# Keys of two latent-attention heads from one product

## The chip, the cores and the metric

The kernel runs on one core of one Trainium2 chip. The metric is the device time of one execution in microseconds (us); lower is better. A change of about 0.5% (6.2 us) is what a measurement of this kernel can tell from no change.

## The reference, cut to what matters

The network has two layers over 256 context and 256 latent tokens, model width 1024. Each layer has three groups of heads (differential attention, multi-head latent attention, a bidirectional recurrence called HGRN2), an output projection and an MLP. The change is in the latent attention (MLA) alone: six heads, whose keys have 64 parts that are made per head from a latent of 128 numbers, and 32 rotary parts that all heads share.

```python
qu = (rmsnorm(cq, g_cq) @ w_uq).reshape(bsz, n, 6, 64 + 32)      # cq: 256 numbers a token
kvu = (rmsnorm(ckv, g_ckv) @ w_ukv).reshape(bsz, n, 6, 64 + 64)  # ckv: 128 numbers a token
q_nope, q_rope = qu[..., :64], qu[..., 64:]
k_nope, mla_v = kvu[..., :64], kvu[..., 64:]
...
s = einsum(q_nope, k_nope) + einsum(q_rope, k_rope)   # k_rope: one for all heads
p = softmax(s * 96 ** -0.5);  o = p @ mla_v
```

In the first layer 512 queries are needed, in the second (last) one only the 256 latent ones.

## The kernel before, in words

Activations lie feature-major: features on the 128 partitions, tokens along the free axis. Most products are made in three parts (`mm3`, L139 to L142): an operand x is split into a high part in the type fp32r and the rest, and high·high, high·low and low·high are added up in PSUM. So a product of 512 tokens is three matmul instructions of 512 columns. The scores (L1225), the turn of the rotary keys (L1171) and the weighting of values (L1239) are plain fp32 products; the trace has two records for each of those.

The stage at hand comes in each layer after the input projections. `do_pair(2)` projects queries and keys of the last pair of differential heads from weights that `wunit` loads into the buffers `raw` (four of them, all loads on SP's queue) and splits into `wh` (ACT, L135) and `wl` (DVE, L136). The MLA weights `w_uq` and `w_ukv` are loaded ahead of that into three of the same `raw` buffers (L1134, L1138) and split into `uqh`, `uql`, `ukh`, `ukl`. Then:

- L1171 turns the shared rotary keys `krt` to partitions 64 to 95 of a PSUM tile, four matmuls; ACT copies them into the lower part of both key buffers `mk` (L1175).
- `mla_head(hd)` (L1177) makes the 64 key parts of one head: three matmuls with 64 stationary columns over 512 tokens, and an ACT copy to `mk` (L1181). Then six matmuls make its 96 query parts, an ACT copy (L1187) takes them to `mq`, and the rotary part of the latent tokens is turned by DVE (L1190) and three POOL operations (L1191 to L1193).
- L1206 to L1208 make the values `mv` of all six heads, twelve matmuls of 384 columns.
- `da_steps` and `mla_steps` give steps of the two attentions in turn, for pairs of heads and blocks of 128 queries. The order of MLA heads is 1, 0, 3, 2, 5, 4; the next head's keys and queries are made half-way through the head before (`s.after`, L1256). A step is scores, maximum (DVE), exponential (ACT), turn (PE, L907), weighted values (L1239).

Between the steps of layer 0 stand matmuls of the modulation of later stages (`mod_group`, L392), as filling work; in layer 1 those of the output projection's last part (`proj_out`). Written order gives priorities; a scheduler that runs when the kernel is built then fixes the order of instructions on each engine.

Of the kernel before, what the change touches and what calls it, by code (L numbers as in the profile page):

```python
# [8 lines left out]
F32 = mybir.dt.float32  # L9
# [13 lines left out]
HALF_TURN = [8 * (i // 8 ^ 1) + i % 8 for i in range(32)]  # L23
# [17 lines left out]
def net(ctx: ExitStack, tc, x, c, cx, c_ctx, w_mod, b_mod, g_mix, g_mlp, w_in, w_out, da_lambda, da_subln_g,  # L41
        g_cq, g_ckv, w_uq, w_ukv, hg_lb, hg_norm_g, w_ff1, w_ff2, g_final,
        k_ident, k_cos, k_sin, k_krc, k_krs, k_mask, out):
    nc = tc.nc
    V, S, G, PE = nc.vector, nc.scalar, nc.gpsimd, nc.tensor
# [10 lines left out]
    ident = const.tile([128, 128], F32, name="ident")  # L56
# [82 lines left out]
    def mm3(ps, lh, ll, rh, rl, start, stop):  # L139
        PE.matmul(ps, lh, rh, start=start, stop=False)  # L140
        PE.matmul(ps, lh, rl, start=False, stop=False)  # L141
        PE.matmul(ps, ll, rh, start=False, stop=stop)  # L142
# [449 lines left out]
    def layer(l):  # L592
        last = l == DEPTH - 1
        T0q = 256 if last else 0
        Tq = NTOK - T0q
# [525 lines left out]
        def split(src, shape, nm):  # L1121
            a = mp.tile(shape, F32R, name=nm + "h")
            b = mp.tile(shape, F32R, name=nm + "l")
            return a, b
# [3 lines left out]
        else:  # L1128
            ukh = wp.tile([128, 1024], F32R, tag="wh", name="ukh", bufs=3)[:, 0:768]
            ukl = wp.tile([128, 1024], F32R, tag="wl", name="ukl", bufs=3)[:, 0:768]  # L1130
        uqh, uql = split(None, [128, 2, 576], "uq")
        for i in range(2):
            raw = raw_tile()[:, 0:576]
            nc.sync.dma_start(out=raw, in_=w_uq[l, 128 * i:128 * i + 128, :])  # L1134
            S.copy(out=uqh[:, i, :], in_=raw)
            V.tensor_sub(out=uql[:, i, :], in0=raw, in1=uqh[:, i, :].bitcast(F32))
        raw = raw_tile()[:, 0:768]
        nc.sync.dma_start(out=raw, in_=w_ukv[l])  # L1138
        S.copy(out=ukh, in_=raw)
        V.tensor_sub(out=ukl, in0=raw, in1=ukh.bitcast(F32))  # L1140

# [25 lines left out]
                return turns[cc][0]  # L1167

        kp = psum("sc")
        for t in range(4):  # L1170
            PE.matmul(kp[64:96, 128 * t:128 * t + 128], krt[:, t, :], ident, start=True, stop=True, tile_position=(0, 64))  # L1171
        NKB = 2
        kbufs = [mp.tile([96, 512], F32, name="mk0"), lp_.tile([128, 512], F32, tag="lat", name="mk1", bufs=3)[0:96, :]]
        for kb in kbufs:
            S.copy(out=kb[64:96, :], in_=kp[64:96, :])  # L1175

        def mla_head(hd, n):  # L1177
            kb = kbufs[n % NKB]
            ps = psum("mm")
            mm3(ps[0:64, :], ukh[:, 128 * hd:128 * hd + 64], ukl[:, 128 * hd:128 * hd + 64], ckh, ckl, True, True)  # L1180
            S.copy(out=kb[0:64, :], in_=ps[0:64, :])  # L1181
            ps = psum("mm")
            cs = slice(96 * hd, 96 * hd + 96)
            for i in range(2):
                mm3(ps[0:96, 0:Tq], uqh[:, i, cs], uql[:, i, cs], cqh[:, i, 0:Tq], cql[i][:, 0:Tq], i == 0, i == 1)
            qb = mp.tile([96, Tq], F32, tag="mq", name="mq", bufs=2)
            S.copy(out=qb[:, 0:Tq], in_=ps[0:96, 0:Tq])  # L1187
            x0 = Tq - 256
            t2 = mp.tile([96, 256], F32, tag="mt2", name="mt2", bufs=2)
            V.stream_shuffle(out=t2[64:96, :], in_=qb[64:96, x0:Tq], mask=HALF_TURN)  # L1190
            G.tensor_mul(out=t2[64:96, :], in0=t2[64:96, :], in1=sinT[64:96, :])  # L1191
            G.tensor_mul(out=qb[64:96, x0:Tq], in0=qb[64:96, x0:Tq], in1=cosT[64:96, :])
            G.tensor_add(out=qb[64:96, x0:Tq], in0=qb[64:96, x0:Tq], in1=t2[64:96, :])  # L1193
            return kb, qb

        heads = {1: mla_head(1, 0)}


        mv = mp.tile([128, 4, 384], F32, name="mv")
        uvh = ukh.rearrange("p (h e) -> p h e", h=6)[:, :, 64:128]  # L1200
        uvl = ukl.rearrange("p (h e) -> p h e", h=6)[:, :, 64:128]
        for t in range(4):
            ps = psum("mm")
            ts = slice(128 * t, 128 * t + 128)
            pv = ps[:, 0:384].rearrange("p (h e) -> p h e", h=6)
            PE.matmul(pv, ckh[:, ts], uvh, start=True, stop=False)  # L1206
            PE.matmul(pv, ckh[:, ts], uvl, start=False, stop=False)
            PE.matmul(pv, ckl[:, ts], uvh, start=False, stop=True)  # L1208
            S.copy(out=mv[:, t, :], in_=ps[:, 0:384])
# [37 lines left out]
        def mla_steps():  # L1247
            order = [1, 0, 3, 2, 5, 4]
            for p in range(3):
                res = {}  # L1250
                for h in (1, 0):
                    for qi, qt in enumerate(qtiles):
                        s = mla_step(p, h, qi, qt, res)
                        n = 2 * p + 1 - h
                        if qi == nq // 2 and n < 5:
                            s.after = lambda n=n: heads.update({order[n + 1]: mla_head(order[n + 1], n + 1)})  # L1256
                        if qi == nq - 1 and h == 0:
                            s.own = [lambda p=p, res=res: (V.reciprocal(out=res["s"], in_=res["s"]),
                                                            turn_y(3 + p, res["o"], res["s"]))]
                        yield s  # L1260
# [183 lines left out]
```

## Time and profile before

| | us |
|---|---|
| three runs | 1239.74, 1242.29, 1244.79 (median 1242.29) |
| the profiled execution | 1242.65 |
| its span in the trace | 1240.9 |
| TensorE busy | 1201.3 (97%) |
| VectorE (DVE) busy | 888.5 (72%) |
| ScalarE (ACT) busy | 584.4 (47%) |
| GpSimd (POOL) busy | 111.4 (9%) |
| attention of layer 0, in the span | about 240 to 372 |
| attention of layer 1, in the span | about 947 to 1035 |

The span is the time from the first to the last instruction of one profiled execution; 1.75 us of its time lie outside. TensorE's busy time counts the modelled ends of pipelined matmuls, so a busy engine may still wait a little.

### The profile page before, as it was taken

The numbers are of one execution on the slowest core, as the hardware profiler recorded it, in microseconds if no ns is written. First come the engines' busy times: TensorE is split into PE (matmuls) and PEld (weight loads), VectorE is DVE, ScalarE is ACT, GpSimd is POOL, SyncE is SP. The second block draws the span as 40 slices with busy tenths as digits, with TensorE's granted clock in tenths as the row PEclk, the third lists the DMA queues.
The fourth block names the chain that finished last, engine by engine and source line by source line (L and its number), as shares of the span: only waits on it lengthen the run. The fifth ranks groups of instructions, "written<-read, shape, count | busy, mean of one in ns | idle before, by whom it ended". The sixth has DMA issues, their size and how long they took to land.

```text
span 1240.9 us, 21471 instructions
## 1 busy us (share of the span) xinstructions
PE 1201.3 (97%) x8318; PEld 963.9 (78%) x8318; DVE 888.5 (72%) x1786; ACT 584.4 (47%) x1114; POOL 111.4 (9%) x156
## 2 busy tenths in 40 slices
PE   6999999999999999999999999999998998999997
PEld 4677888755568777878787877788986668999997
DVE  4675587767776997765778673796788877865864
ACT  3534344576653654211233322464347874653653
POOL 2200000221200100000000000140003421000000
PEclk9999999999999999999999999999999998999999
DMA  9631213456543346555555554233324413555662
GB/s 324 187 86 49 76 53 105 119 158 198 189 153 107 98 139 198 188 154 159 178 155 162 164 169 134 68 103 99 94 58 121 126 32 119 175 184 187 187 187 69
DMA packets 138199, 170.93 MB, mean 138 GB/s; under 512 B 10883, under 2 KB 116033, under 8 KB 138097
## 3 DMA queue, kind: packets, MB, share of 16 engines
q1 hardware_dynamic: 134816, 164.08, 43.8%
q0 software_dynamic: 2704, 4.94, 1.6%
q8 instruction: 66, 1.08, 0.4%
q10 hardware_dynamic: 576, 0.53, 0.1%
q14 instruction: 37, 0.30, 0.1%
HBM read 160.21 MB, written 1.05 MB: 130 GB/s over the span
## 4 chain that ended last, share of the span: by engine, by line
PE 85%; DVE 7%; DMA 3%; ACT 3%; POOL 1%; issue 1%; ACTq 0%; POOLq 0%; SPq 0%
PE mm L142 21%; PE mm L140 21%; PE mm L141 21%; PE sc L1239 3%; PE sc L1225 2%; PE mm L392 2%; PE tp L907 2%; PE mm L219 2%; PE mm L218 2%; PE mm L220 2%; DMA mraw<-in_w_mod_dram 2%; PE sc L797 1%; DMA raw<-in_w_in_dram 1%; PE mm L930 1%; DVE wl L136 1%; PE sc L691 1%
## 5 line engine op out<-in xcount | busy, mean ns | idle before, releaser
L135 ACT CAST wh<-raw 128x1024 fp32r<-128x1024 f32 (+2 forms) x204 | 211.0, 1035 | 315.4 <-PE mm L141 244.9
L136 DVE TENSOR_TENSOR wl<-raw,wh 128x1024 fp32r<-128x1024 f32 (+2 forms) x201 | 242.9, 1209 | 127.5 <-ACT wh L135 124.7
L140 PE MATMUL mm<-mhh,wh 128*128 128x512 f32 (+1 forms) x512 | 174.0, 340 | 0.8 <-DVE fz L336 0.8
L140 PE MATMUL mm<-fa,wh 128*128 128x512 f32 (+1 forms) x512 | 173.7, 340 | 0.0
L142 PE MATMUL mm<-mhh,wl 128*128 128x512 f32 (+1 forms) x512 | 173.0, 339 | 0.4 <-DVE wl L136 0.4
L141 PE MATMUL mm<-mhl,wh 128*128 128x512 f32 (+1 forms) x512 | 173.3, 338 | 0.0
L141 PE MATMUL mm<-fb,wh 128*128 128x512 f32 (+1 forms) x512 | 173.3, 339 | 0.0
L142 PE MATMUL mm<-fa,wl 128*128 128x512 f32 (+1 forms) x512 | 173.2, 339 | 0.0
L426 DVE SCALAR_TENSOR_TENSOR room<-raw,scm,room 128x1024 f32<-128x1024 f32 x84 | 106.4, 1287 | 39.8 <-DMA raw<-in_w_mod_dram 39.8
L140 PE MATMUL mm<-hh,wh 128*128 128x512 f32 (+1 forms) x336 | 126.7, 382 | 4.6 <-ACT hh L351 3.3
L141 PE MATMUL mm<-hl,wh 128*128 128x512 f32 (+1 forms) x336 | 126.8, 378 | 2.3 <-DVE hl L352 2.3
L142 PE MATMUL mm<-hh,wl 128*128 128x512 f32 (+1 forms) x336 | 126.8, 378 | 1.1 <-DVE wl L136 1.1
L140 PEld LDWEIGHTS mm<-mhh,wh 128*128 128x128 f32 x512 | 96.2, 188 | 15.5 <-ACT wh L135 2.5
L140 PEld LDWEIGHTS mm<-fa,wh 128*128 128x128 f32 x512 | 96.3, 188 | 14.2 <-ACT wh L135 2.5
L142 PEld LDWEIGHTS mm<-mhh,wl 128*128 128x128 f32 x512 | 96.3, 188 | 12.5 <-DVE wl L136 0.8
L142 PEld LDWEIGHTS mm<-fa,wl 128*128 128x128 f32 x512 | 96.4, 188 | 11.7
L141 PEld LDWEIGHTS mm<-fb,wh 128*128 128x128 f32 x512 | 96.5, 189 | 11.6
L141 PEld LDWEIGHTS mm<-mhl,wh 128*128 128x128 f32 x512 | 96.3, 188 | 11.2
L140 PEld LDWEIGHTS mm<-hh,wh 128*128 128x128 f32 x336 | 63.5, 190 | 15.6 <-ACT hh L351 4.2
L141 PEld LDWEIGHTS mm<-hl,wh 128*128 128x128 f32 x336 | 64.2, 191 | 14.0 <-DVE hl L352 4.1
L142 PEld LDWEIGHTS mm<-hh,wl 128*128 128x128 f32 x336 | 64.0, 191 | 13.2 <-DVE wl L136 2.0
L347 POOL TENSOR_TENSOR nt<-nt,bc 128x256 f32<-128x256 f32 x24 | 27.0, 1132 | 493.5 <-ACT bc L326 445.5
(333 smaller groups left out, 2189.8 us busy)
## 6 DMA issues: line engine op xcount, KB each, us to landing
raw<-in_w_ff_dram SPq DMA_DIRECT2D x128, 512.0 KB, 3.8
raw<-in_w_mod_dram SPq DMA_DIRECT2D x80, 512.0 KB, 3.7
raw<-in_w_in_dram SPq DMA_DIRECT2D x42, 512.0 KB, 3.8
mraw<-in_w_mod_dram SPq DMA_DIRECT2D x32, 256.0 KB, 6.0
raw<-in_w_out_dram SPq DMA_DIRECT2D x10, 512.0 KB, 3.7
raw<-in_w_in_dram SPq DMA_DIRECT2D x16, 256.0 KB, 5.1
raw<-in_w_in_dram SPq DMA_DIRECT2D x8, 384.0 KB, 3.3
K<-dah POOLq DMA_DIRECT2D x48, 64.0 KB, 2.3
```

Of the source, the lines that this page charges most:

```text
L135: S.copy(out=wh, in_=raw)
L136: (low.pop() if low else V).tensor_sub(out=wl, in0=raw, in1=wh.bitcast(F32))
L140: PE.matmul(ps, lh, rh, start=start, stop=False)
L141: PE.matmul(ps, lh, rl, start=False, stop=False)
L142: PE.matmul(ps, ll, rh, start=False, stop=stop)
L218: PE.matmul(ps, a, wh[:, k, 0:w], start=st, stop=False)
L219: PE.matmul(ps, a, wl[:, k, 0:w], start=False, stop=False)
L220: PE.matmul(ps, b, wh[:, k, 0:w], start=False, stop=sp)
L347: G.tensor_mul(out=ts, in0=ts, in1=self.bc[:, a - T0:b - T0])
L392: PE.matmul(ps[32 * j:32 * j + 32, :], scm[:, k, :], raw[:, 512 * q:512 * q + 512], start=(k == 0), stop=(k == KT - 1))
L426: V.scalar_tensor_tensor(out=acc[r], in0=raw, scalar=scm[:, k, r:r + 1], in1=acc[r], op0=ALU.mult, op1=ALU.add)
L1239: PE.matmul(op[64 * r:64 * r + 64, 0:128], v[:, j, 64 * c:64 * c + 64], PT[:, js], start=(j == 0), stop=(j == nk - 1), tile_position=(0, 6 ...
```

## The change

The keys of the two heads of a pair now come out of one product with 128 stationary columns (`mla_keys`), three matmuls for two heads. The even head has its 64 key parts on partitions 0 to 63 and the rotary part on 64 to 95, as before. The odd head has its key parts on partitions 64 to 127, its rotary part on 32 to 63, and zeros on 0 to 31; its scores are a product over 128 rows. So the rotary keys are turned twice (eight matmuls), and one more ACT copy and a clearing of 32 rows are there. The queries of an odd head are made with 128 stationary columns. For that the weights are loaded in another order of columns: each half of `w_uq` by three DMAs of pieces of 96, 32 and 64 columns, `w_ukv` by two DMAs of 64 columns a head, all keys ahead of all values; the values' weights are then one contiguous operand of 384 columns.

```diff
         for i in range(2):
             raw = raw_tile()[:, 0:576]
-            nc.sync.dma_start(out=raw, in_=w_uq[l, 128 * i:128 * i + 128, :])
+            rv = raw.rearrange("p (n f) -> p n f", n=3)
+            wv = w_uq[l, 128 * i:128 * i + 128, :].rearrange("p (n f) -> p n f", n=3)
+            for o, a, b in ((0, 0, 96), (96, 160, 192), (128, 96, 160)):
+                nc.sync.dma_start(out=rv[:, :, o:o + b - a], in_=wv[:, :, a:b])
...
         raw = raw_tile()[:, 0:768]
-        nc.sync.dma_start(out=raw, in_=w_ukv[l])
+        wv = w_ukv[l].rearrange("p (h f) -> p h f", h=6)
+        for o in (0, 384):
+            nc.sync.dma_start(out=raw[:, o:o + 384].rearrange("p (h f) -> p h f", h=6), in_=wv[:, :, o // 6:o // 6 + 64])
...
-        for t in range(4):
-            PE.matmul(kp[64:96, 128 * t:128 * t + 128], krt[:, t, :], ident, start=True, stop=True, tile_position=(0, 64))
-        NKB = 2
-        kbufs = [mp.tile([96, 512], F32, name="mk0"), lp_.tile([128, 512], F32, tag="lat", name="mk1", bufs=3)[0:96, :]]
-        for kb in kbufs:
+        for r in (64, 32):
+            for t in range(4):
+                PE.matmul(kp[r:r + 32, 128 * t:128 * t + 128], krt[:, t, :], ident, start=True, stop=True, tile_position=(0, r))
+        keven = [mp.tile([96, 512], F32, name="mk0"), lp_.tile([128, 512], F32, tag="lat", name="mk1", bufs=3)[0:96, :]]
+        kodd = mp.tile([128, 512], F32, name="mk2")
+        for kb in keven:
             S.copy(out=kb[64:96, :], in_=kp[64:96, :])
-
-        def mla_head(hd, n):
-            kb = kbufs[n % NKB]
+        S.copy(out=kodd[32:64, :], in_=kp[32:64, :])
+        V.memset(kodd[0:32, :], 0.0)
+
+        def mla_keys(p):
+
+            cs = slice(128 * p, 128 * p + 128)
             ps = psum("mm")
-            mm3(ps[0:64, :], ukh[:, 128 * hd:128 * hd + 64], ukl[:, 128 * hd:128 * hd + 64], ckh, ckl, True, True)
-            S.copy(out=kb[0:64, :], in_=ps[0:64, :])
+            mm3(ps, ukh[:, cs], ukl[:, cs], ckh, ckl, True, True)
+            S.copy(out=kodd[64:128, :], in_=ps[64:128, :])
+            S.copy(out=keven[p % 2][0:64, :], in_=ps[0:64, :])
+
+        def mla_head(hd):
+
+            p, odd = hd // 2, hd % 2
+            n, r = (128, 32) if odd else (96, 64)
             ps = psum("mm")
-            cs = slice(96 * hd, 96 * hd + 96)
+            cs = slice(192 * p + 64 * odd, 192 * p + 64 * odd + n)
...
-                            s.after = lambda n=n: heads.update({order[n + 1]: mla_head(order[n + 1], n + 1)})
+                            def after(n=n):
+                                if n % 2:
+                                    mla_keys(n // 2 + 1)
+                                heads[order[n + 1]] = mla_head(order[n + 1])
+                            s.after = after
```

How the instructions move on the engines (line numbers from L1135 on shift between the two kernels). First ACT at the start of layer 1's attention, before: `yh` is a part of the output projection's operand, `mk` with numbers 9059 and 9060 are the two key buffers, `sc` and `mm` are PSUM tiles.

```order
L1001 ACTIVATE yh<-tp,vT_91 128x256 x2
L1175 COPY mk_9059<-sc 32x512
L1181 COPY mk_9059<-mm 64x512
L1175 COPY mk_9060<-sc 32x512
L1187 COPY mq<-mm 96x256
L1209 COPY mv<-mm 128x384 x4
```

The same place of the changed kernel, where 9070 is the odd heads' buffer, 9068 and 9069 the even ones':

```order
L1001 ACTIVATE yh<-tp,vT_91 128x256 x2
L1182 COPY mk_9068<-sc 32x512
L1191 COPY mk_9070<-mm 64x512
L1182 COPY mk_9069<-sc 32x512
L1183 COPY mk_9070<-sc 32x512
L1192 COPY mk_9068<-mm 64x512
L1203 COPY mq<-mm 128x256
L1226 COPY mv<-mm 128x384 x4
```

Five copies instead of three stand ahead of the first queries' copy `mq`. Next ACT some 20 us earlier in layer 1, while HGRN2 ends and `do_pair(2)` takes its weights, as one piece of the difference: `wh` is the split of its first weights, `dah`, `rx` and `dak` are parts of the differential attention, `ktok` of HGRN2.

```order
-L135 CAST wh<-raw 128x1024
+L873 CAST dah<-dak 128x512
 L764 COPY ktok<-tp 128x256
-L873 CAST dah<-dak 128x512
-L855 ACTIVATE rx<-mm 128x256
-L853 ACTIVATE dak<-mm 128x256
+L855 ACTIVATE rx<-mm 128x256
+L135 CAST wh<-raw 128x1024
 L798 COPY obuf<-sc 128x2x128
```

The split of these weights moved behind three other ACT operations. Last PE in layer 1 where the keys and queries of head 0, the second head, are made, and the transposed probabilities `P` (differential) and `mP` (MLA) follow; before:

```order
L142 MATMUL mm<-yh,wl 128x256
L140 MATMUL mm<-ckh,ukh 64x512
L141 MATMUL mm<-ckl,ukh 64x512
L142 MATMUL mm<-ckh,ukl 64x512
L140 MATMUL mm<-cqh,uqh 96x256
L907 MATMUL tp<-ident,P 128x128 x4
L907 MATMUL tp<-ident,mP 128x128 x4
L141 MATMUL mm<-cql,uqh 96x256
L142 MATMUL mm<-cqh,uql 96x256
```

and in the changed kernel:

```order
L142 MATMUL mm<-yh,wl 128x256
L140 MATMUL mm<-cqh,uqh 96x256
L141 MATMUL mm<-cql,uqh 96x256
L142 MATMUL mm<-cqh,uql 96x256
L140 MATMUL mm<-cqh,uqh 96x256
L141 MATMUL mm<-cql,uqh 96x256
L142 MATMUL mm<-cqh,uql 96x256
L930 MATMUL mm<-K_8837,Q_8836 128x512 x2
L907 MATMUL tp<-ident,P 128x128 x4
L907 MATMUL tp<-ident,mP 128x128 x4
```

The three matmuls of the keys are gone there, and all queries of head 0 are made ahead of the turns of `P` and `mP`. Outside the two attention stages and the work just ahead of them the rows of both kernels are alike.

## Rows read from the trace of the kernel before

**Rows 1.** Busy time by stage: length, PE, PEld, DVE, ACT, POOL, PEclk, DMA, GB/s.
```profile
240.00:372.00 132.00, 131.45 (x838) 77.04 (x837) 92.61 (x257) 88.06 (x257) 25.02 (x42) 1.00 0.55 168
956.00:1035.00 79.00, 70.70 (x507) 51.79 (x508) 62.00 (x161) 58.59 (x149) 30.23 (x43) 0.97 0.30 84
```
**Rows 2.** Waits of PE, 240 to 372 and 900 to 1060 us: total, times, longest.
```profile
PE mm L140 <- ACT P L936: 0.4, 1, 0.4
...
PE sc L1225 <- POOL mq L1193: 4.3, 5, 1.5
PE tp L901 <- DVE P L898: 4.2, 1, 4.2
```
**Rows 3.** Timeline of PE, start of layer 0's attention: start, duration, instruction.
```profile
240.23 1.06 PE L1171 MATMUL sc<-ident,krt 128*32 128x128 f32 x8
...
241.74 0.39 PE L142 MATMUL mm<-ckh,ukl 128*64 128x512 f32 x1
241.97 0.39 PE L140 MATMUL mm<-cqh,uqh 128*96 128x512 f32 x1
242.19 0.39 PE L141 MATMUL mm<-cql,uqh 128*96 128x512 f32 x1
...
243.33 0.34 PE L1206 MATMUL mm<-ukh,ckh 128*128 128x384 f32 x1
243.51 0.34 PE L1207 MATMUL mm<-ukl,ckh 128*128 128x384 f32 x1
```
**Rows 4.** The chain that ended last, start of layer 1's attention: start, length, what.
```profile
949.77 0.28 ACT dak L853
...
951.08 0.58 ACT mk L1175
...
952.89 0.38 ACT mq L1187
```
**Rows 5.** Timeline of SP's queue, layer 1: first start, time until the last issue ends.
```profile
927.38 7.24 SPq L130 DMA_DIRECT2D raw<-in_w_in_dram  x2
```
**Rows 6.** Timelines of ACT, DVE and PE, layer 1; idle time before in brackets.
```profile
931.91 1.05 ACT L135 CAST wh<-raw 128x1024 fp32r<-128x1024 f32 x1 [0.72 <-DMA raw<-in_w_in_dram]
...
932.99 1.23 DVE L136 TENSOR_TENSOR wl<-raw,wh 128x1024 fp32r<-128x1024 f32 x1 [1.23 <-ACT wh L135]
...
933.13 0.62 ACT L873 CAST dah<-dak 128x512 fp32r<-128x512 f32 x1
933.65 0.39 ACT L855 ACTIVATE rx<-mm 128x256 f32<-128x256 f32 x1
...
942.15 0.50 PE L142 MATMUL mm<-hh,wl 128*128 128x512 f32 x1 [0.24 <-DVE wl L136]
...
947.05 0.39 PE L142 MATMUL mm<-hh,wl 128*128 128x512 f32 x1
...
966.56 1.13 PE L1225 MATMUL sc<-mk,mq 96*128 96x512 f32 x2 [1.02 <-POOL mq L1193]
```
**Rows 7.** The page, part 6: DMA issues, size of each, median us to landing.
```profile
raw<-in_w_in_dram SPq DMA_DIRECT2D x42, 512.0 KB, 3.8
...
raw<-in_mla_w_ukv_dram SPq DMA_DIRECT2D x2, 384.0 KB, 3.8
...
raw<-in_w_in_dram SPq DMA_DIRECT2D x8, 32.0 KB, 3.1
```
**Rows 8.** Busy time by stage, end of layer 1's attention; columns as in rows 1.
```profile
1032.00:1036.00 4.00, 3.57 (x17) 3.60 (x18) 1.80 (x6) 1.12 (x3) 0.00 (x0) 0.50 0.46 135
1036.00:1040.00 4.00, 4.00 (x31) 4.00 (x30) 2.78 (x5) 2.51 (x6) 0.00 (x0) 0.84 0.00 0
```
**Rows 9.** Timelines of POOL and DVE just ahead of that.
```profile
1026.14 2.38 POOL L136 TENSOR_TENSOR wl<-raw,wh 128x1024 fp32r<-128x1024 f32 x1 [5.60 <-ACT wh L135]
...
1026.27 2.27 DVE L234 SCALAR_TENSOR_TENSOR rs_t<-rs 128x4 f32<-128x4 f32 x1
...
1029.17 2.19 DVE L235 TENSOR_TENSOR rs_t<-rs_t,rs_m 128x4 f32<-128x4 f32 x1
```

More of the change, by code (lines that the diff above doesn't have):

```diff
@@ L1182, in mla_head @@
+        def mla_head(hd):
+            p, odd = hd // 2, hd % 2
+            n, r = (128, 32) if odd else (96, 64)
             ps = psum("mm")
-            cs = slice(96 * hd, 96 * hd + 96)
+            cs = slice(192 * p + 64 * odd, 192 * p + 64 * odd + n)
             for i in range(2):
-                mm3(ps[0:96, 0:Tq], uqh[:, i, cs], uql[:, i, cs], cqh[:, i, 0:Tq], cql[i][:, 0:Tq], i == 0, i == 1)
-            qb = mp.tile([96, Tq], F32, tag="mq", name="mq", bufs=2)
-            S.copy(out=qb[:, 0:Tq], in_=ps[0:96, 0:Tq])
+                mm3(ps[0:n, 0:Tq], uqh[:, i, cs], uql[:, i, cs], cqh[:, i, 0:Tq], cql[i][:, 0:Tq], i == 0, i == 1)
+            qb = mp.tile([128, Tq], F32, tag="mq", name="mq", bufs=2)
+            S.copy(out=qb[0:n, 0:Tq], in_=ps[0:n, 0:Tq])
@@ L1188, in mla_head @@
             x0 = Tq - 256
[L1189 to L1196, printed above, removed]
+            t2 = mp.tile([128, 256], F32, tag="mt2", name="mt2", bufs=2)
@@ L1199, in layer @@
+            rs = slice(r, r + 32)
+            V.stream_shuffle(out=t2[rs, :], in_=qb[rs, x0:Tq], mask=HALF_TURN)
+            G.tensor_mul(out=t2[rs, :], in0=t2[rs, :], in1=sinT[rs, :])
+            G.tensor_mul(out=qb[rs, x0:Tq], in0=qb[rs, x0:Tq], in1=cosT[rs, :])
+            G.tensor_add(out=qb[rs, x0:Tq], in0=qb[rs, x0:Tq], in1=t2[rs, :])
+            return kodd if odd else keven[p % 2], qb[0:n, :]
+        mla_keys(0)
+        heads = {1: mla_head(1)}
         mv = mp.tile([128, 4, 384], F32, name="mv")
-        uvh = ukh.rearrange("p (h e) -> p h e", h=6)[:, :, 64:128]
@@ L1201, in layer @@
-        uvl = ukl.rearrange("p (h e) -> p h e", h=6)[:, :, 64:128]
+        uvh, uvl = ukh[:, 384:768], ukl[:, 384:768]
         for t in range(4):
@@ L1204, in layer @@
             ts = slice(128 * t, 128 * t + 128)
-            pv = ps[:, 0:384].rearrange("p (h e) -> p h e", h=6)
+            pv = ps[:, 0:384]
             PE.matmul(pv, ckh[:, ts], uvh, start=True, stop=False)
```

## The prediction

> **What bounds the kernel now.** I read the busy times by stage first, then the waits of PE, then the chain and the timelines at the places that the change touches. In the attention of layer 0 PE is busy for 131.45 of 132 us, DVE for 92.61, ACT for 88.06 [rows 1], and PE's only listed wait there is one of 0.4 us [rows 2]. The reader is to see that in this stage PE's work is the time, since the filling matmuls of the modulation take up what the two attentions leave. In the attention of layer 1 PE is busy for 70.70 of 79 us [rows 1]: it waits 4.3 us in five waits for POOL's rotation of MLA queries, and 4.2 us in one wait for DVE at the end [rows 2]. So there a time comes from a latency (matmul, ACT copy, DVE, three POOL operations, scores) at the start of a head as often as from PE's work. A microsecond saved on PE counts fully in layer 0 and in part in layer 1.
>
> **What the change removes.** Three key matmuls per pair and layer: 9 a layer. A matmul of 512 columns lasts 0.39 us by its record, but the next one starts 0.23 us later (241.74, 241.97), and that spacing is the price [rows 3]. 9 x 0.23 = 2.07 us a layer.
>
> **What it adds on PE.** Four more matmuls a layer for the second turn of the rotary keys, 8 records. The 8 records of now take 1.06 us together [rows 3], the last one's modelled end included, so 1.06 us a layer is the upper end, and I take it; somewhat less is possible, nothing is not. Wider stationary operands I cost at nothing: 64 columns and 96 columns both start 0.23 and 0.22 us apart for 512 moving columns, and 128 columns start 0.18 us apart for 384 (0.47 ns a column against 0.45) [rows 3]. That the values' weights become contiguous could give at most the difference, 0.02 ns x 384 x 12 = 0.1 us; I take 0. The scores of an odd head over 128 instead of 96 rows: no row shows fp32 scores over 128 rows; the nearest is the turn of the rotary keys, an fp32 product over 128 rows whose 8 records of 128 columns take 1.06 us, 1.04 ns a column [rows 3]; the scores over 96 rows take 1.13 us for two records of 512, 1.10 ns a column [rows 6]. Rows of the array make no difference there; I take 0 from either end.
>
> **Layer 0** is then -2.07 + 1.06 = -1.01 us. What could eat it: two more ACT copies stand ahead of the first queries' copy. PE has the twelve matmuls of the values to do meanwhile (12 x 0.18 = 2.1 us [rows 3]), which hides 2 x 0.58 us. Without that cover it would be +1.16.
>
> **Layer 1, its start.** Here ACT ends the chain: from 949.77 on it works without a pause up to the copy `mq` at 952.89 [rows 4], and scores of head 1 wait for what follows. The row order shows five copies instead of three ahead of `mq`; one takes 0.58 us [rows 4], so head 1 starts 2 x 0.58 = 1.16 us later. Behind the copies on ACT stand the values' copies and the first exponentials, which go later by as much. The second turn's 1.06 us on PE lies ahead of that, where PE waits for a weight split anyway (below), and costs nothing. The clearing of 32 rows on DVE stands in a stretch in which ACT, not DVE, ends the chain; I take 0, and 0.3 us if that cover is gone.
>
> **Layer 1, the later heads.** Head 0: PE waited 1.02 us for POOL ahead of its scores [rows 6]. Now its three key matmuls and its `mk` copy are gone, and its queries are made ahead of the turns of `P` and `mP` instead of around them. The chain to the scores starts by more than 1.02 us earlier against its neighbours, so that wait goes: -1.02. Heads 2 and 4: 6 key matmuls gone, 6 x 0.23 = 1.38 us of PE; between none (latency bound) and all (PE bound) I take half, -0.70, since PE's share of this stage's time is high but five waits for POOL are on the chain. Heads 3 and 5 have one `mk` copy more ahead of `mq`, heads 2 and 4 one less: +1.16 and -1.16 at most, taken as 0. Sum of layer 1: +1.16 - 1.02 - 0.70 = -0.56 us; the bounds are +1.9 (the wait stays and the matmuls save nothing, with 0.3 for DVE and 0.4 of copies) and -2.4 (the late start is made up by DVE's and ACT's slack too).
>
> **The loads.** `w_uq` comes in 1152 pieces of 128 to 384 bytes a half instead of 128, `w_ukv` in 1536 of 256 bytes. No row shows such a load; the nearest are 256 pieces of 128 bytes that land in 3.1 us and 1024 pieces of 512 bytes in 3.8 us, and the old `w_ukv` in 3.8 [rows 7]. So the new `w_ukv` lands between 0 and 3.8 x 1536 / 1024 - 3.8 = 1.9 us later. In layer 1 `w_ukv` itself is issued ahead of the loads at 927.38 [rows 5], and its split stands among the last ACT operations before 949.77 [rows 4], so it can be some 10 us late; in layer 0 the same splits are done before PE, without a wait, reaches them at 241 [rows 3]. What it is moved ahead of on SP's queue counts: the two loads of `do_pair(2)` in layer 1. The first of these was taken by ACT the moment it landed (a wait of 0.72 us for the DMA [rows 6]). The row order moves that split behind two operations of 0.62 and 0.39 us [rows 6], so the first 1.0 us of a late landing costs nothing; but the split itself is 1.0 us later for that order alone. The second load is issued when the first's `wl` is done (932.99 + 1.23 = 934.2, and SP's two issues end at 927.38 + 7.24 = 934.6) [rows 5, 6], since the MLA weights hold the three other buffers. So it comes 1.0 us later, and with it PE's matmul that waited 0.24 us for its `wl` at 942.15 [rows 6]. PE then ends these products at 947.05 + 0.39 + 1.0 = 948.4, and the first that reads them is ACT at 949.77 [rows 4, 6]. So up to 1.3 us more is hidden; I take 0, bound 0.6 (1.9 later less 1.3). The Trainium skill, "DMA: Bandwidth & Descriptors", section "Specifications", says that a transfer needs pieces of at least 512 bytes for full rate and that shorter ones cost a read-modify-write; its rule speaks against this change. No row here shows the rate of such pieces beyond the 32 KB load; if they moved at half the rate, the 384 KB would, as an estimate, take about 1 us longer, still under that cover, and the sum would stay.
>
> **Sum.** -1.01 - 0.56 = -1.57 us. Against the profiled execution's 1242.65 (a span of 1240.9 and 1.75 around it) this is 1241.1. The median of the runs is 0.36 lower than that execution; the forecast stays at 1241.1, a change of 0.1%.
>
> **Rivals.**
> - *The removed products were never the bound.* If the scheduler's new order fills layer 0 no better and layer 1 is all latency, nothing comes of the 18 matmuls: -1.01 falls to about 0, layer 1 gives +0.5. For it: layer 1's waits for POOL. Against it: 0.4 us of waits in layer 0. Time 1243.
> - *Faster: the end of layer 1's attention falls into place.* There two splits on POOL of about 2.4 us each hold up two small DVE operations (2.27 and 2.19 us for 4 numbers a row) [rows 9], PE waits 4.2 us [rows 2], and then its granted clock is 0.50, the lower level of 1.2 GHz, for 4 us and 0.84 for the next 4 [rows 8], which loses 4 x 0.5 + 4 x 0.16 = 2.6 us. If the DVE chain came about 1.2 us earlier against POOL's splits it would miss the second: -2.2, and with a shorter wait the clock might stay up: -2.6. Time 1241.1 - 4.8 = 1236.3. Against it: ACT's order there is unchanged, and both start from the same copies.
> - *Slower: the start of layer 1 with the clock.* The pieces land 1.9 us late, the split order adds 1.0, PE waits over 2 us ahead of 942, then again for ACT around 955; if these empty stretches come near the 4.2 us after which the clock was at 0.50 [rows 2, 8], the same 2.6 us are lost, besides 0.6 of late products and head 0's wait that stays (1.02). That is 1241.1 + 4.2 = 1245.3; with layer 1 at its other bound (1.9 + 0.56 in place of the 1.02) 1246.7. Against it: PE's clock is at 1.0 there now. The Trainium skill, "TensorE: Matmul & The Clock Gate", section "Part 1", has the half clock as the state that idleness brings and work releases; the trace agrees with 0.50 after the wait of 4.2 us.
>
> **Chances.** The forecast 0.62, the first rival 0.14, faster 0.11, slower 0.13. A change by 0.5% is 6.2 us, which is what a measurement can tell: below 1236.1 lies the better half of the faster rival and some unforeseen gain from the new order (0.10 together), above 1248.5 only a slower rival with more than one such loss (0.07); the rest, 0.83, is no change. The range reaches to the rivals, 1236.4 to 1246.4, and leaves out about 2 in 10. The forecast and the first rival alone lie within 1238.5 to 1243.5.
>
> **What would show it.** In the profile after: 18 fewer key matmuls and 16 more records of the turn; layer 0's attention about 1.0 us shorter with PE's waits there still under 1 us; in layer 1 head 1's `mq` copy about 1.2 us later against HGRN2's last output, the wait for POOL ahead of head 0's scores gone, `wl` of the last pair's second load about 1 us later; the wait of 4 us and the half clock at the end still there. The prediction is wrong if PE waits in layer 0 for a copy or a buffer (the odd heads' single key buffer), if the loads in small pieces land over 3 us later, or if the granted clock falls at a place where it is 1.0 now.

## The result: slower by 0.65%, most of it in layer 0

The changed kernel takes 1251.59 us (median of 6 runs, 1249.76 to 1252.92) against 1243.49 for the kernel before: a ratio of 1.0065, 95% interval 1.0049 to 1.0081, or 8.1 us more. Its profiled execution took 1251.86 us, with a span of 1250.1. The forecast was 1241.1, no change, with a range up to 1246.4: wrong.

**Where the time goes.** The row order outside the two attentions is alike, so the same instruction can be sought in both traces. First the timelines of DVE, before (columns: start, duration, instruction, idle time ahead of it with what ended it):

```profile
235.99 0.42 DVE L860 TENSOR_TENSOR daq<-rs,rx 128x256 f32<-128x256 f32 x1
...
371.18 1.23 DVE L136 TENSOR_TENSOR wl<-raw,wh 128x1024 fp32r<-128x1024 f32 x1 [2.00 <-PE mm L142]
```

and the same two of the changed kernel:

```profile
234.94 0.43 DVE L860 TENSOR_TENSOR daq<-rs,rx 128x256 f32<-128x256 f32 x1
...
377.27 1.23 DVE L136 TENSOR_TENSOR wl<-raw,wh 128x1024 fp32r<-128x1024 f32 x1 [2.81 <-PE mm L142]
```

The changed kernel comes in 1.05 us early and goes out 6.09 late: the attention of layer 0 lost 7.1 us. From there on everything stands 6.1 us later up to about 930 us; the attention of layer 1 adds 2.4 to 2.8 more in this execution.

The two attentions after, by stage (length, PE, PEld, DVE, ACT, POOL, PEclk, DMA, GB/s; the first two rows answer to [rows 1], the others are the start and the end of layer 1's attention, which answers to [rows 8]):

```profile
239.00:378.00 139.00, 138.07 (x837) 79.20 (x836) 93.00 (x257) 89.22 (x258) 25.05 (x42) 1.00 0.52 160
963.00:1044.00 81.00, 70.23 (x502) 52.46 (x502) 62.40 (x162) 58.59 (x149) 31.73 (x42) 0.95 0.31 89
...
944.00:956.00 12.00, 10.66 (x69) 8.85 (x68) 11.47 (x33) 7.10 (x17) 0.77 (x2) 1.00 0.40 114
956.00:968.00 12.00, 8.56 (x45) 6.25 (x44) 8.64 (x22) 11.46 (x27) 5.12 (x9) 1.00 0.31 80
...
1040.00:1044.00 4.00, 3.20 (x15) 3.23 (x16) 2.17 (x7) 1.12 (x3) 0.00 (x0) 0.51 0.40 135
```

In layer 0 PE is as busy as before, at the full clock, with the same number of records (837, and 838 in [rows 1]), and yet takes 7 us more. Its waits in layer 0 (239 to 378 us) are still under 1 us:

```profile
PE tp L901 <- DVE spare L898: 0.5, 1, 0.5
PE mm L930 <- ACT spare L936: 0.4, 1, 0.4
```

So nobody is waited for: the same matmuls take longer. Groups of PE's instructions in that stage show which. The filling matmuls of the modulation before, and after (count, busy time and mean ns, idle time ahead):

```profile
L392 PE MATMUL mm<-raw,scm 128*32 128x512 f32 x128 | 28.5, 605 | 0.0
```

```profile
L392 PE MATMUL mm<-raw,scm 128*32 128x512 f32 x128 | 33.7, 605 | 0.0
```

The same 128 records of the same 605 ns keep PE busy for 5.2 us more. A timeline of PE after shows how (a fill is four matmuls with 32 stationary columns each, which write four different quarters of the PSUM tile's rows; two records each; the first row is the turn of the rotary keys and answers to [rows 3]):

```profile
239.18 1.53 PE L1178 MATMUL sc<-ident,krt 128*32 128x128 f32 x16
...
249.27 1.05 PE L392 MATMUL mm<-raw,scm 128*32 128x512 f32 x2
250.25 0.44 PE L907 MATMUL tp<-ident,P 128*128 128x128 f32 x2
250.52 0.38 PE L907 MATMUL tp<-ident,mP 128*128 128x128 f32 x2
250.83 1.06 PE L392 MATMUL mm<-raw,scm 128*32 128x512 f32 x6
251.82 0.73 PE L930 MATMUL mm<-K,Q 96*128 96x512 f32 x2
...
254.52 0.43 PE L1256 MATMUL sc<-PT,dav 128*64 128x128 f32 x2
254.88 1.04 PE L392 MATMUL mm<-raw,scm 128*32 128x512 f32 x2
255.86 0.66 PE L907 MATMUL tp<-ident,P 128*128 128x128 f32 x4
256.44 0.32 PE L1256 MATMUL sc<-mPT,mv 128*64 128x128 f32 x1
256.45 0.32 PE L1256 MATMUL sc<-PT,dav 128*64 128x128 f32 x1
```

and before, in the same part of the stage:

```profile
257.33 1.06 PE L392 MATMUL mm<-raw,scm 128*32 128x512 f32 x8
258.33 0.50 PE L930 MATMUL mm<-K,Q 96*128 96x256 f32 x2
```

One matmul alone (2 records) holds PE for 0.98 us, three for 0.99, four for 1.00: those that stand next to each other run at once, and a group costs the same whatever its size. Before, the 64 matmuls stand in 27 such groups; in the changed kernel in 32, because the scheduler put other instructions between them. The products with the values do the same in twos, with 64 columns each; in the last rows of the changed kernel's timeline a differential product `PT` went ahead by itself at 254.52, and its MLA partner `mPT` came 1.9 us later. Adding up, over the stage, the distance from each record's start to the next record's start (us, worked out from PE's whole timeline):

| | before | after | |
|---|---|---|---|
| filling matmuls | 26.6 | 31.5 | +4.9 |
| products with values | 22.9 | 24.9 | +2.0 |
| turns of `P` and `mP` | 16.2 | 17.6 | +1.4 |
| differential scores | 14.4 | 15.2 | +0.8 |
| MLA keys | 5.1 | 2.8 | -2.3 |
| MLA queries, MLA scores | 24.8 | 24.5 | -0.3 |
| turn of the rotary keys | 1.0 | 1.5 | +0.5 |
| whole stage, the rest included | 135.0 | 142.2 | +7.1 |

The keys give what was forecast; the fillers and value products that were taken apart cost three times that. Why the turns and the differential scores take 2.2 us more isn't shown.

**Layer 1.** PE's waits there after (930 to 1060 us; total, times, longest; these answer to [rows 2]):

```profile
PE sc L1242 <- POOL mq L1210: 6.1, 5, 1.8
PE tp L901 <- DVE P L898: 4.3, 1, 4.3
PE mm L142 <- DVE wl L136: 2.0, 2, 1.1
```

The waits for the turned queries grew from 4.3 to 6.1 us, and those for weight splits from 0.24 [rows 6] to 2.0. Something else is in this execution too: the granted clock fell late in this attention, by stage as above:

```profile
1004.00:1008.00 4.00, 2.27 (x18) 1.95 (x18) 3.93 (x10) 3.65 (x11) 2.38 (x3) 1.00 0.00 0
1008.00:1012.00 4.00, 4.00 (x23) 2.91 (x24) 3.27 (x10) 1.64 (x6) 1.46 (x3) 0.67 0.00 0
1012.00:1016.00 4.00, 4.00 (x25) 2.21 (x24) 1.60 (x3) 3.60 (x11) 1.04 (x1) 0.91 0.00 0
```

For part of the last 8 us the engine ran at its lower level, 1.2 GHz, after a stretch in which PE was busy for 2.27 of 4 us. That is worth up to 4 x 0.33 + 4 x 0.09 = 1.7 us of the 2.4 to 2.8. The kernel with the change in layer 0 alone (below) shows 0.57 from 1008 to 1012 us with the old code in layer 1, and the one with the change in layer 1 alone stays at 1.00 there, so the fall doesn't go with the change in layer 1; and the mean granted clock of the changed kernel's six executions, 0.990 to 0.994, is within that of the kernel before, 0.989 to 0.995. What layer 1 costs is better read from the runs.

### The profile page after: what moved, and what is told of

It reads as the page before. It is cut to its first block, busy times and chain, and to the rows that moved or that the text cites. A ratio compares the mean times of both kernels' runs of the same rounds, so it can differ in the third digit from the quotient of the medians.

```text
span 1250.1 us, 21496 instructions
## 1 busy us (share of the span) xinstructions
PE 1206.8 (97%) x8316; PEld 967.1 (77%) x8316; DVE 889.6 (71%) x1788; ACT 586.2 (47%) x1116; POOL 113.1 (9%) x156
## 3 DMA queue, kind: packets, MB, share of 16 engines
HBM read 160.21 MB, written 1.05 MB: 129 GB/s over the span
## 4 chain that ended last, share of the span: by engine, by line
PE 85%; DVE 9%; ACT 3%; POOL 2%; issue 1%; DMA 1%; SPq 0%; POOLq 0%; ACTq 0%; DVEq 0%
PE mm L140 21%; PE mm L142 21%; PE mm L141 20%; PE sc L1256 3%; PE mm L392 2%; PE sc L1242 2%; PE tp L907 2%; PE mm L218 2%; PE mm L219 2%; PE mm L220 2%; PE sc L797 1%; DVE wl L136 1%; PE mm L930 1%; PE sc L768 1%; PE sc L691 1%
## 5 line engine op out<-in xcount | busy, mean ns | idle before, releaser
L140 PEld LDWEIGHTS mm<-hh,wh 128*128 128x128 f32 x336 | 63.5, 190 | 16.2 <-ACT hh L351 4.0
```

## The experiments

Two theories. **Packing**: the change is close to neutral by its own work, and the time is lost because the scheduler's new order takes apart matmuls that ran at once on different columns of the array. **Own work or loads**: the new copies, the second turn, the wider products or the loads in small pieces cost the time. Unless said otherwise a figure in us is the ratio to the kernel before, timed beside it, times its 1243 us.

**One layer at a time.** The loads, the turns, the heads and the hook of the change stand under a condition on the layer (`last` for layer 1, `not last` for layer 0), those of before under its `else`:

```diff
+        if last:
...
+            mla_keys(0)
+            heads = {1: mla_head(1)}
...
+        else:
...
+            heads = {1: mla_head(1, 0)}
```

Layer 1 alone: 

> The change in layer 1 alone; layer 0 keeps the old code. The theory (packing): most of the loss arises in layer 0, where the trace of the changed kernel falls back by 7.1 us between 235 and 370 us, since the filling matmuls of the modulation stand in 32 groups on TensorE instead of 27, and a group takes 0.98 us whether it has two records or eight; layer 1 falls back by 2.4 to 2.8 us. So this kernel is 2.4 to 2.8 us slower than before. Rival (loads): the weights in small pieces cost the time wherever someone waits for them, and SP's queue is waited for in layer 1 only; then this kernel is 6 us or more slower. Rival (own work): the second turn and the wider products cost alike in both layers; then it is about half of the 8 us slower, some 4.

Layer 0 alone: 

> The change in layer 0 alone; layer 1 keeps the old code. The theory (packing): 5 more groups of filling matmuls at 0.98 us, 2.0 us for value products that no longer stand in pairs, 2.2 us for turns and differential scores, 2.3 us less for keys: 6 to 7 us slower than before. Rival (loads): the weights are split long before TensorE reaches them in layer 0, so no change within 1 us. Rival (own work): some 4 us slower.

Measured: layer 1 alone 1.0015 (1.0006 to 1.0024), 1.9 us; layer 0 alone 1.0057 (1.0043 to 1.0072), 7.1 us. Together 9.0, against 8.1 for the whole change. Layer 1 is a little under the 2.4 to 2.8 that was expected, with an interval from 0.7 to 3.0 us. Most of the loss is in layer 0, as the trace had it, and against the rivals' splits; it doesn't yet say why.

**The fillers held together.** In the function that makes them both loads are issued first; the products of the second load go first, and an ordering edge with a raised priority lets the other three follow at once:

```diff
+    def chained(made):
+        for a, b in zip(made, made[1:]):
+            behind(a, b)
...
+            raws = [raw_tile() for _ in range(2)]
...
+            first = mod_mm(2)
+            with tc.high_priority():
+                chained([first] + [mod_mm(j) for j in (3, 0, 1)])
-                for q in range(2):
-                    j = 2 * hf + q
-                    PE.matmul(ps[32 * j:32 * j + 32, :], scm[:, k, :], raw[:, 512 * q:512 * q + 512],
...
```

In the kernel before: 

> The kernel before, with the four filling matmuls of a step (four times 32 columns of the array) held together on TensorE: both loads are issued first, the products of the second load go first, and the other three follow at once. Row order: 16 groups instead of 27. The theory (packing): 11 x 0.98 = 10.8 us faster than before. Rival: TensorE is busy in layer 0 only by the modelled ends, and what is freed there turns into waits for DVE, ACT or the loads; then 0 to 3 us faster.

In the changed kernel: 

> The changed kernel with the same hold: 16 groups instead of 32. The theory (packing): 16 x 0.98 = 15.7 us faster than the changed kernel, that is some 7 us faster than before, and 3 to 4.5 us slower than the kernel before with the same hold (what layer 1 and the other pieces of layer 0 cost). Rival (own work or loads): the hold gives both kernels the same, so that this one stays 8 us behind the other held one.

Measured: 0.9911 (0.9896 to 0.9925), 11.1 us faster than before, where 10.8 was worked out from the number of groups; and 0.9940 (0.9925 to 0.9955), 7.5 us faster than before and so about 15.5 faster than the changed kernel, where 15.7 was worked out. A group in the held kernel before:

```profile
254.17 1.07 PE L400 MATMUL mm<-raw,scm 128*32 128x512 f32 x8
255.17 0.50 PE L942 MATMUL mm<-K,Q 96*128 96x256 f32 x2
```

The gain comes whole, so PE's work is the bound of layer 0 indeed; but its size is the number of groups, not of matmuls. The two held kernels stand 3.6 us apart instead of 8.1.

**The value products held together as well**, in turn, the later MLA one first:

```diff
-                    for PT, v, c, r in ((d.PT, dav, 2 * p + 1 - h, 1 - h), (s.PT, mv, hd, h)):
+                todo = [(j,) + x for j in range(nk) for x in ((s.PT, mv, hd, h), (d.PT, dav, 2 * p + 1 - h, 1 - h))]
+                first = val_mm(*todo[0])
+                with tc.high_priority():
+                    chained([first] + [val_mm(*x) for x in todo[1:]])
```

> The kernel before with the filling matmuls held together, and also the products of both attentions' probabilities with their values, which use 64 columns of the array each: the MLA one goes first, the differential one follows at once, in turn. The theory (packing): in layer 0 the 288 records of these products take 22.9 us by their starts; wholly in pairs (1.02 us for a step of 8 pairs, 0.6 for one of 4) they would take 19.4, so this kernel is 3.4 us faster than with the fillers alone, 14 to 15 us faster than before. Rival: the hold makes the differential product wait for the MLA turn, and what is gained is lost in waits; then 10 to 11 us faster than before, as with the fillers alone.

> The changed kernel with both holds. The theory (packing): its value products took 24.9 us in layer 0, so it gains 5.4 us over the fillers alone, and layer 0 of both held kernels is then equal within 1 us; what is left is layer 1's 1.9 us and this kernel is 1 to 2.5 us slower than the other held one. Rival (own work): it stays 3.6 us behind, as with the fillers alone.

Measured: 0.9870 (0.9855 to 0.9885) and 0.9869 (0.9854 to 0.9884), 1226.64 and 1226.71 us. Both are 16 us faster than the kernel before, the fastest versions of this study, and they are equal within intervals of 1.9 us either way. Here the value products take 19.9 and 20.3 us in layer 0, by the sum over starts as above. So with the groups whole, the change costs and gains nothing that can be measured; the expected 1 to 2.5 us of layer 1 are not there either.

**The copies and the loads on top of that.** First the even heads' copies written behind the queries:

```diff
-        for kb in keven:
-            S.copy(out=kb[64:96, :], in_=kp[64:96, :])
         S.copy(out=kodd[32:64, :], in_=kp[32:64, :])
...
-        mla_keys(0)
+        even = mla_keys(0)
         heads = {1: mla_head(1)}
+        for kb in keven:
+            S.copy(out=kb[64:96, :], in_=kp[64:96, :])
+        even()
```

> The changed kernel with both holds, and ACT's copies in another written order: ahead of the first queries' copy stand three copies (the odd heads' rotary part and key part, one even rotary part) instead of five, and the even head's key part follows the queries in later pairs too. If the two extra copies at the start of layer 1 cost 0.6 to 1.2 us, as forecast, this kernel is that much faster than the changed kernel with both holds. Rival (the shuffle of the queries on DVE stands behind other DVE work anyway, or the loads are what is late): no difference beyond 0.3 us.

Then, with the copies as they were, whole loads (`w_ukv` likewise):

```diff
-            for o, a, b in ((0, 0, 96), (96, 160, 192), (128, 96, 160)):
-                nc.sync.dma_start(out=rv[:, :, o:o + b - a], in_=wv[:, :, a:b])
+            nc.sync.dma_start(out=raw, in_=w_uq[l, 128 * i:128 * i + 128, :])
```

> The changed kernel with both holds, with the MLA weights loaded whole as before the change. The columns then stand in the old order, so that the heads are made from other columns of the weights; all operations keep their shapes. If the loads in small pieces cost nothing, as forecast, the time is that of the changed kernel with both holds within 0.5 us. Rival (loads): the second load of the last pair of differential heads, which was issued 8.3 us later by the clock where its neighbours were 6.1 us later, comes back by 1 to 2 us, and this kernel is 1 to 2 us faster.

Measured: neither gains. With the copies later 1228.16 us, 0.9876 (0.9860 to 0.9893); with whole loads 1227.67, 0.9878 (0.9863 to 0.9893). They are 1.5 and 1.0 us above 1226.71, within the intervals. With the copies later, PE's waits for the turned queries in layer 1 are no shorter (4.0 us in four waits, 3.6 in four without that edit), and those for DVE's `P` grew (7.9 us in four waits, from 5.4 in two).

**Whether it is the columns.**

```diff
-                return PE.matmul(ps[32 * j:32 * j + 32, :], scm[:, k, :], raws[j // 2][:, 512 * (j % 2):512 * (j % 2) + 512],
-                                 start=(k == 0), stop=(k == KT - 1))
+                return PE.matmul(ps, ones, raws[j // 2][:, 512 * (j % 2):512 * (j % 2) + 512],
+                                 start=(k == 0 and j == 2), stop=(k == KT - 1 and j == 1))
```

> The kernel before with the four filling matmuls held together, as in the earlier run, but each with a stationary operand of 128 columns (a tile of ones) in place of its own 32, so that no two of them use different columns of the array. The modulation that comes out is not the reference's; the number of matmuls, their 512 moving columns and their places are the same. If the four run at once because they stand side by side on different columns (the theory), they now run one behind the other: the second pass of one starts 0.45 us after its first, so a group takes 4 x 0.91 instead of 0.98 us, and the kernel is 16 x 2.66 = some 43 us slower than with the hold alone (1231), that is some 1274. Rival (standing next to each other is enough, whatever the columns): 1231.

Measured: 1.0195 (1.0175 to 1.0215), 1265.27 us, 34 us above the kernel with the hold alone, where 43 was expected. Its timeline of PE:

```profile
254.35 3.59 PE L400 MATMUL mm<-raw,ones 128*128 128x512 f32 x8
257.78 0.60 PE L919 MATMUL tp<-ident,P 128*128 128x128 f32 x4
```

The same four matmuls, side by side but on all columns, hold PE for 3.43 us instead of 1.00. By 16 groups that is some 39 us; the value products happen to be taken apart less in this order (48 unbroken runs for 57), which gives some of it back (20.4 us by starts for 23.2). Standing next to each other is not enough; the columns must differ.

**One part undone: each head makes its own keys.** No hold here; the rest of the change stays.

```diff
+        def mla_head(hd):
+            p, odd = hd // 2, hd % 2
+            o = 64 * odd
+            cs = slice(128 * p, 128 * p + 64 + o)
+            ps = psum("mm")
+            mm3(ps[0:64 + o, :], ukh[:, cs], ukl[:, cs], ckh, ckl, True, True)
+            S.copy(out=(kodd if odd else keven[p % 2])[o:o + 64, :], in_=ps[o:o + 64, :])
```

> The changed kernel, without any hold, with one part undone: each head makes its own keys again, just ahead of its queries (the odd head by the product of 128 columns of which only the upper half is copied, the even one by 64 columns), so 9 matmuls a layer are back. Loads in pieces, odd heads' rows, second turn and extra copies stay. Row order: 27 groups of fillers (changed kernel 32, before 27), values in 52 unbroken runs (changed 62, before 56). The theory (packing): although it does more work than the changed kernel, it is 6 to 9 us faster than that, within 2.5 us of before. Rival (own work, loads or copies): it is 1 to 3 us slower than the changed kernel, since it has all of its costs and the 18 matmuls besides.

Measured: 0.9985 (0.9973 to 0.9997), 1240.74 us. With 18 matmuls more than the changed kernel, and with its loads, second turn and copies, it is 10 us faster than that, a little more than expected, and no slower than before. In its trace the fillers stand in 27 groups and take 26.6 us by starts, as before the change. This is the plainest case against the rivals: what the shared product saves is small, and what its place in the order breaks up is large.

**The loads alone, in the kernel before** (`w_ukv` likewise, by two DMAs):

```diff
-            nc.sync.dma_start(out=raw, in_=w_uq[l, 128 * i:128 * i + 128, :])
+            for a, b in ((0, 96), (96, 128), (128, 192)):
+                nc.sync.dma_start(out=rv[:, :, a:b], in_=wv[:, :, a:b])
```

> The kernel before with the MLA weights loaded in the pieces of the change (three DMAs for a half of the queries' weights, two for the keys' and values'), each to the old place of its columns. Row order: 27 groups of fillers as before, values in 59 runs for 56. If the loads cost nothing, as forecast, it is within 1.5 us of before. Rival (loads): 2 us slower or more, of which the start of layer 1 has most.

Measured: 1.0003 (0.9994 to 1.0013). The loads in pieces cost nothing that can be measured here, -0.7 to 1.6 us. In the changed kernel the two DMAs of `w_ukv`, 192 KB each, land after a median of 3.6 us (4.5 in this run); the single one of before, 384 KB, took 3.8 [rows 7]. They do leave a trace in layer 1. SP's queue in this run, the two loads of `do_pair(2)`, and PE's waits:

```profile
925.55 8.47 SPq L130 DMA_DIRECT2D raw<-in_w_in_dram  x2
```

```profile
PE mm L142 <- DVE wl L136: 1.7, 2, 0.9
PE mm L140 <- ACT wh L135: 0.9, 1, 0.9
```

The second load is issued 1.2 us later behind the first (8.47 us for both instead of 7.24 [rows 5]): it waits for DVE's part `wl` of the first one's split, which starts 1.9 us after ACT's `wh` here, behind other operations of DVE, and started 1.1 us after it before [rows 6]. PE then waits 2.6 us for splits of weights where it waited 0.24 [rows 6]. In return a wait of the kernel before, some 7 us behind that, is gone, for the split of the latent `ckh`:

```profile
PE mm L140 <- ACT ckh L1144: 1.3, 1, 1.3
```

**Layer 1 by itself.** Its 1.9 us had no cause in the groups: the row order breaks none there. Two kernels with the change in layer 1 alone, with the edits that were shown above, the copies behind the queries in one and whole loads in the other, in layer 1's branch only:

> The change in layer 1 alone, as in the first run (1.9 us slower than before), with three of ACT's copies ahead of the first queries' copy instead of five. If the two extra copies are what layer 1 loses, as the prediction's term of 1.16 us had it, this kernel is 1.0 to 1.9 us faster than the first run, at before within 1 us. Rival (loads: the last projections' weights come later): it stays 1.5 to 2 us slower than before.

> The change in layer 1 alone with its MLA weights loaded whole, the columns in the old order, so that the heads of layer 1 are made from other columns of the weights; all operations keep their shapes. If the loads are what layer 1 loses, this kernel is 1 to 1.9 us faster than the first run. Rival (the copies and the order of the later heads): no difference from the first run beyond 0.5 us.

Measured: with three copies ahead of the queries 0.9972 (0.9958 to 0.9986), 3.5 us faster than before and 5 us faster than the first run, more than either theory expected. With whole loads 1.0006 (0.9995 to 1.0017). That is 1.1 us faster than the first run by the ratios, as the theory of the loads has it, and yet within the noise of either; PE's 2.0 us of waits for `wl` are gone in it, those for the turned queries are 5.1 us instead of 6.1. So this run doesn't decide between the two. PE's waits in layer 1 of the first run and of the one with the copies later:

```profile
PE sc L1285 <- POOL mq L1219: 6.1, 5, 1.8
```

```profile
PE sc L1290 <- POOL mq L1221: 2.2, 3, 0.9
```

The longest of these waits stood ahead of head 3. There ACT had both key copies ahead of the queries in the first run, and a weight split of 1.06 us ahead of those:

```profile
974.61 0.59 ACT L909 COPY mPT<-tp 128x512 f32<-128x512 f32 x1
975.09 1.06 ACT L135 CAST wh<-raw 128x1024 fp32r<-128x1024 f32 x1
...
976.85 0.58 ACT L1200 COPY mk<-mm 64x512 f32<-64x512 f32 x1
977.44 0.58 ACT L1201 COPY mk<-mm 64x512 f32<-64x512 f32 x1
977.92 0.36 ACT L1212 COPY mq<-mm 128x256 f32<-128x256 f32 x1
```

and with the copies later, the even one and the split stand behind:

```profile
971.64 0.59 ACT L909 COPY mPT<-tp 128x512 f32<-128x512 f32 x1
972.42 0.58 ACT L1198 COPY mk<-mm 64x512 f32<-64x512 f32 x1 [0.20 <-PE mm L142]
...
973.71 0.36 ACT L1214 COPY mq<-mm 128x256 f32<-128x256 f32 x1
973.97 0.58 ACT L1201 COPY mk<-mm 64x512 f32<-64x512 f32 x1
974.44 1.05 ACT L135 CAST wh<-raw 128x1024 fp32r<-128x1024 f32 x1
```

The waits ahead of heads 1, 3 and 5 went from 1.13, 1.81 and 1.73 us to 0.51, none and none. From the copy `mPT` to the queries' copy ahead of head 3 it is 3.31 us in the first run and 2.07 with the copies later; before the change it was 0.96, with one key copy and no split between. In the first run the split takes 0.95 us of that by starts, the second key copy 0.48. So layer 1 loses by what stands on ACT ahead of the queries, and the copies are a part of it; the edit changed the order of other instructions too, and gave more than the change had lost, so that the share of the copies isn't shown. Where all products were held together, the same edit gave nothing; there the waits for the turned queries were already short (3.6 us), and no split stands between `mPT` and the queries' copy of head 3.

## Why the prediction was wrong

**The step that failed** is the first: "in this stage PE's work is the time, since the filling matmuls of the modulation take up what the two attentions leave", and from it that layer 0 changes by what is removed and added, -2.07 + 1.06. That PE is the bound was right: every microsecond of groups saved on it came through (10.8 worked out, 11.1 measured). What failed is that the work of the untouched matmuls was held constant. A busy share of 131.45 in 132 us [rows 1] doesn't tell one matmul that holds the array from four that share it. The row order shows the broken groups without any run (27 against 32), and I read it only where keys and queries stood. None of the rivals had it: the slower one looked for the loss in layer 1 and in the clock. Of the three signs named as those of a wrong prediction one came, the granted clock of 0.67 at a place where it was 1.00, which isn't shown to come of the change; PE waits for no key buffer in layer 0, and no load of the changed kernel lands 3 us later.

**The terms that were right.** The keys: -2.07 forecast, -2.3 by starts. Wider stationary operands and scores over 128 rows: 0, measured -0.3 together. The contiguous weights of the values: 0, their products take 2.12 us by starts in both kernels. The second turn: 1.06 was given as an upper end; 16 records last 1.53 us where 8 took 1.06 [rows 3], so 0.5. The extra copies in layer 0: hidden, since no wait for them is listed. The loads: 0, a ratio of 1.0003 measured; the second split of `do_pair(2)` is later than its neighbours by 2.2 us instead of 1.0 (ACT's `wh` at 947.38, at 939.07 before, where other work stands 6.1 later), and ACT's split of the MLA weights behind it is not later for that. So PE waits longer for it, and less for what comes after it. The Trainium skill, "DMA: Bandwidth & Descriptors", section "Specifications", asks for pieces of at least 512 bytes for the full rate. No run here shows a time lost by it: the two DMAs of `w_ukv`, half the bytes each, land 3.2 to 3.7 us after their issue, the whole one 3.5 to 4.1.

**The terms that were mis-sized.** With the groups whole, the change in layer 0 is worth +0.1 us in the two traces (ACT goes from 0.65 to 0.56 us ahead between 234 and 364 us), not -1.01; with a difference of medians of 0.07 us the whole change is neutral where -1.57 was forecast. By starts the keys give 2.8 us there, and the rotary keys (0.5), the turns of `P` and `mP` (1.2), the scores of both attentions (0.6) and the values (0.4) take it back; the forecast had only the keys and the rotary keys. The start of layer 1 was put at +1.16: five copies of `mk` take 2.63 us up to `mq` where three took 1.81, so +0.8, and the scores of head 1 start 0.4 us later than the work around. For heads 3 and 5 one copy more ahead of `mq` was "taken as 0": the waits ahead of their scores are 1.81 and 1.73 us with the change in layer 1, where they were 0.46 and 1.48, and none with the copies later. Head 0's wait of 1.02 us [rows 2, 6] was forecast to go and is 0.85: its queries' copy ends on ACT at 968.88, but DVE's shuffle of them starts at 970.36, behind a reduction of scores and the scaling of `P` that DVE has ahead in the row. Layer 1 measured by itself is +1.9 us (0.7 to 3.0) instead of -0.56, at the bound that the prediction gave.

**The rivals.** Faster: the wait of 4.2 us at the end of layer 1 is still there (4.3), and the clock of 0.51 behind it, 1.2 GHz. Slower, with the clock: at the start of layer 1's attention (944 to 968 us) the granted clock stays at 1.00, the 2.4 GHz level; it fell later, at 1008. First rival, that nothing comes of the removed matmuls: true in effect once the groups are whole, though its reason was another one.

**Open.** Why the shared keys make the scheduler place five more breaks isn't shown; only that a kernel with the keys apart has none of them. In layer 1 the shares of the copies, of the split and of the late loads aren't parted. In the kernels with both holds PE waits 3.2 and 3.6 us there for the turned queries, 0.4 us apart where it was 1.8, which goes with the loss that vanishes; why the order comes out so isn't shown.

## What to carry to other kernels

Before counting a saved matmul on a busy engine, look in its timeline for records that start a few ns apart: their price is that of the group, and an edit nearby that moves one of them out costs a whole one. Count such groups in the row order of both kernels, over the whole stage and not only where the edit stands; where they are the bound, tie them together with ordering edges, which here made either kernel 16 us faster than the one before. And a copy that isn't needed by the next product may be worth placing behind the one that is: with its effects on the order it gave 5 us in one kernel here and nothing in another.

## What the runs showed of the hardware

Matmuls on different columns of the array start 6 to 7 ns apart when they stand next to each other: four of 32 columns and 512 moving columns in fp32 take 1.00 us together, one takes 0.98, and four on all 128 columns take 3.43 to 3.54. So four on different columns are 3.4 to 3.5 times as fast as four on the same ones. The Trainium skill, "TensorE: Matmul & The Clock Gate", section "Part 3: Packing small matmuls — row/col tiling", has such a group last as long as one matmul and about 4 ns for each further one; the traces agree, with 6 to 7 ns. The value products of a step, 16 records in 8 pairs of 64 columns each, take 1.02 us in most steps of the held kernel.
